# Neighbourhood attention inside a fused block: TensorE in a written order, six filling units a step

## The chip, the core and the metric

The kernel runs on one NeuronCore of a Trainium2 chip. A core has five engines that run side by side: TensorE (PE in the profile, with its weight loads as PEld), VectorE (DVE), ScalarE (ACT), GpSimd (POOL) and SyncE (SP), which here issues the transfers. Each engine takes its instructions in the fixed order in which the program was written out for it; between engines there are semaphores. The metric is the time of one execution on the device, in microseconds (us), the median of several runs; lower is better.

## The reference, cut to what matters

One layer of a diffusion backbone on 1024 latent tokens (a grid of 16 rows by 64 columns) with 256 context tokens, 1024 features, all in fp32. The stage that matters here is the neighbourhood attention, beside the wide projections that are independent of it:

```python
h = modulate(rmsnorm(x, norm1_g), sh1, sc1)
q, k, v = ...                      # 8 heads of 64, q and k normalised
s_loc = einsum(q, k_window) * scale + bias      # 8 x 16 window round each query
s_ctx = einsum(q, k_ctx) * scale                # all 256 context keys
p = softmax(concat([s_loc, s_ctx]))             # one softmax over both
o_na = p_loc @ v_window + p_ctx @ v_ctx
og, m_a, m_b = h @ w_in[:, ...]                 # 2560 further columns: "dense" products
o_g = gla_bidir(...)                            # chunked linear attention, next stage
mix = (sigmoid(m_a) * (o_na @ w_br_na) + sigmoid(m_b) * (norm(o_g) * silu(og) @ w_br_gla)) @ w_out
```

## The kernel before

Every fp32 product is made of three products of fp32r parts (high and low halves). The stages follow each other: input norms and projections, neighbourhood attention (NA), linear attention (GLA), merge of the two branches, output projection, feed-forward network.

**The filler.** The 2560 columns of og, m_a and m_b need 320 *units*: a unit is three products of 128x512 into the bank `psd` (one feature block `k` of one output tile). They depend on nothing in the attention, so a generator (`dense_units`, `fill(n)`) hands them out n at a time wherever TensorE would otherwise wait. Eight units make a tile, which ACT (and DVE for og) takes out of PSUM as `std`. NA and GLA take fixed numbers of units; what is left over is written out in one block by `fill(1000)` (line 1008) between GLA and the merge.

**NA.** 8 heads x 4 steps, a step being two query tiles of 128 ("piece", `c2`). What a step does is set by the words of `ORD` (line 48), read in `na_out` (lines 754 to 766). `tN`: group N of four 128x128 blocks of the probabilities `pb` is transposed on TensorE into a bank `pt`; ACT casts it to `phl` (high part) and DVE subtracts for the low part. `aN`: the value products of that group, `pv<-phl,vhl`. A step has 9 or 10 blocks, so groups 0 and 1 are full and group 2 has one or two. `l`: the logits of the **next** step (`cp` for the context, `lp` for the window, two tiles each). `w`: its softmax: DVE takes the minimum `mn` and, with the bias, `pb` and `mx`; ACT takes four exponentials with their sums; DVE adds and inverts the sums (`rs`); DVE scales the first tile's `pb` and ACT the second's. `fN`: N units. `p`: transposes of the next head's keys and queries (`tpk`, `tpq`), two groups in the first two steps of a head, one in the third, none in the fourth. `pt`, `tpk` and `tpq` share two PSUM banks (tag "T", `bufs=2`), which come free when DVE has read them. At the end of a step ACT and DVE add the two halves of `pv` (`t1n`), and DVE adds the result into `oT`, whose two inputs lie in SBUF.

**What sets the order.** With `in_order(True)` each TensorE instruction is tied to the one written before it. With `in_order(False)` a scheduler chooses when the program is built, by its own estimate of times; the chosen order is then as fixed on the chip as a written one. GLA and the merge are in a written order in both kernels; NA's is `NAO` (line 792), and before NA comes the start: keys and queries of head 0, eight units (`FSTART`, line 790), the first logits and softmax (line 791).

```python
prepare(0, 9)
prepare(1, 1)
fill(FSTART)
cur = na_weights(0, 0, *na_logits(0, 0))
in_order(NAO)
for s, (h, c2) in enumerate(steps):
    ...
    cur = na_out(h, c2, steps[s + 1] if s + 1 < len(steps) else None, *cur)
```

**After GLA.** The merge needs `ona_d` (NA's output, written to HBM) and `w_na` back in SBUF as four and two pages of high and low parts (lines 1083 to 1088): a page is loaded by SP into `raw` (three buffers, shared with GLA), cast by ACT (`w_hi`), and subtracted on DVE (`w_lo`). Its products go to the bank `psb`.

Of the kernel before, what the change touches and what calls it, by code (L numbers as in the profile page):

```python
# [43 lines left out]
OORD = (0, 0, 1, 1)  # L44
FIN = 2
NPB = 3
NAO = False
ORD = "f2 t0 l t1 w f1 a0 t2 f1 a1 f1 a2 p".split()
FG = 0
FSTART = 8  # L50
PREP = (2, 2, 2, 0)
# [37 lines left out]
def hybrid_block_kernel(  # L89
# [35 lines left out]
    class Ordered:  # L125
# [4 lines left out]
        def in_order(self, on):  # L130
            self.on, self.last = on, None
# [502 lines left out]
    with ExitStack() as sn:  # L634
# [48 lines left out]
        def na_logits(h, c2):  # L683
            bias, vhl, qh, ql, ks = heads[h]
            cp = nps.tile([P, 2, TC], F32, tag="C", name="cp")
            for ci in range(2):
                cs_ = slice((2 * c2 + ci) * P, (2 * c2 + ci + 1) * P)
                PE.matmul(cp[:, ci], qh[:, cs_], ks[:, T:], start=True, stop=False)
                PE.matmul(cp[:, ci], ql[:, cs_], ks[:, T:], start=False, stop=True)
            lps = []  # L690
            for ci in range(2):
                c = 2 * c2 + ci
                k0, k1 = max(0, c - 1), min(8, c + 2)
                nl = (k1 - k0) * P
                lp = nps.tile([P, 512], F32, tag="L", name="lp", bufs=2)
                cs_ = slice(c * P, (c + 1) * P)
                PE.matmul(lp[:, 0:nl], qh[:, cs_], ks[:, k0 * P:k1 * P], start=True, stop=False)
                PE.matmul(lp[:, 0:nl], ql[:, cs_], ks[:, k0 * P:k1 * P], start=False, stop=True)
                lps.append((lp, k0, k1, nl))
            return cp, lps  # L700
# [32 lines left out]
        def na_out(h, c2, ahead, blocks, pbs, ns):  # L733
# [19 lines left out]
            res = None  # L753
            for op in ORD:
                if op[0] == "f":
# [35 lines left out]
# [3 lines that stand above are left out]
# [930 lines left out]
```

## Time and profile before

| | us |
|---|---|
| median of 3 runs (1607.38 to 1611.16) | 1608.04 |
| the profiled execution's own time | 1602.4 |
| its span, first to last instruction | 1600.6 |
| start of NA's transposes to the last value product | 355.2 to 595.3 |
| GLA with its units | 595.3 to 734.2 |
| the left-over units | 734.2 to 759.6 |
| merge, from its first product | 759.6 |

TensorE is busy in 96% of the span. Busy time of TensorE is a model of pipelined products, whose ends overlap; so a waiting time that the profile shows is somewhat shorter than what the engine lost.

### The profile page before, as it was taken

Reading aid. Unit: us, or ns where it says so; the run is one execution under the profiler, and the core shown is the slowest. Engines: PE = TensorE matmul, PEld = TensorE weight load, DVE = VectorE, ACT = ScalarE, POOL = GpSimd, SP = SyncE. Lnnn points to the kernel's source line nnn. Section 1 sums busy time; section 2 is a strip of 40 time slices with the busy share of each in tenths; the row PEclk is TensorE's granted clock in tenths of the full one; section 3 lists DMA queues with packets and bytes.
Section 4 is the critical chain, followed back from the end, with each engine's and each line's share of the span. In section 5 each row is a group of like instructions: output and inputs, shape, how many; then the busy total and the mean of one; then the engine's idle time right before and its main releaser. Section 6 shows DMA issues by size and latency. Waiting matters only on the chain.

```text
span 1600.6 us, 21607 instructions
## 1 busy us (share of the span) xinstructions
PE 1535.6 (96%) x7884; PEld 1257.4 (79%) x7884; DVE 1017.5 (64%) x1598; ACT 637.8 (40%) x1221; POOL 516.4 (32%) x340
## 2 busy tenths in 40 slices
PE   6998999999989999999999999799999999999998
PEld 4777777888878787778878887688888888877886
DVE  5745567228877865543684678866666665768356
ACT  4333453248777763122212434233333333344442
POOL 3333000023121211210221421655555555245444
PEclk9999999999999999999999999999999999999999
DMA  9456576454333327415652343433333333874342
GB/s 339 127 174 210 170 250 211 154 156 124 112 105 94 98 88 228 151 67 204 225 182 66 106 132 106 138 115 116 99 99 99 99 112 119 269 250 145 99 145 99
DMA packets 171668, 235.50 MB, mean 147 GB/s; under 512 B 15581, under 2 KB 105629, under 8 KB 171561
## 3 DMA queue, kind: packets, MB, share of 16 engines
q1 hardware_dynamic: 171560, 234.11, 45.2%
q8 instruction: 62, 1.02, 0.3%
q14 instruction: 46, 0.37, 0.1%
HBM read 167.83 MB, written 66.24 MB: 146 GB/s over the span
## 4 chain that ended last, share of the span: by engine, by line
PE 71%; DVE 12%; DMA 5%; issue 5%; ACT 4%; POOL 2%; SPq 1%; ACTq 0%; DVEq 0%; POOLq 0%
PE psdn L137 10%; PE psj L137 9%; PE psd L137 9%; PE fZ L137 7%; PE fW L137 7%; PE fX L137 6%; PE pso L137 5%; PE psb L137 4%; PE fY L137 4%; PE pv L137 2%; PE pt L137 1%; SPq L137 1%; ACT pb L137 1%; POOL r L249 1%; PE mp L137 1%
## 5 line engine op out<-in xcount | busy, mean ns | idle before, releaser
L137 PE MATMUL psdn<-wd,a 128*128 128x512 f32 x924 | 213.4, 392 | 5.0 <-ACT u L137 2.0
L137 PEld LDWEIGHTS psdn<-wd,a 128*128 128x128 f32 x924 | 174.0, 189 | 44.3 <-DVE a L137 3.4
L211 POOL TENSOR_TENSOR w_P<-sc,w_P 128x512 fp32r<-128x512 f32 x80 | 119.4, 1495 | 126.3 <-ACT w_P L137 126.3
L137 PE MATMUL fZ<-T,w_P 128*128 128x512 f32 x528 | 128.3, 392 | 8.5 <-DVE u L137 8.5
L137 PE MATMUL psd<-hh,w_hi 128*128 128x512 f32 x320 | 133.6, 418 | 0.0
L211 POOL TENSOR_TENSOR w_lo<-raw,w_hi 128x1024 fp32r<-128x1024 f32 x24 | 57.6, 2404 | 219.9 <-ACT w_hi L137 195.1
L137 PE MATMUL psd<-hh,w_lo 128*128 128x512 f32 x320 | 128.1, 400 | 0.0
L137 PE MATMUL psj<-w_hi,hh 128*128 128x512 f32 x320 | 127.0, 399 | 0.7 <-ACT hh L137 0.6
L137 PE MATMUL psd<-hl,w_hi 128*128 128x512 f32 x320 | 127.3, 398 | 0.0
L137 PE MATMUL psj<-w_lo,hh 128*128 128x512 f32 x320 | 126.0, 394 | 0.0
L137 PE MATMUL psj<-w_hi,hl 128*128 128x512 f32 x320 | 125.3, 395 | 0.3 <-DVE r L137 0.3
L137 PEld LDWEIGHTS fZ<-T,w_P 128*128 128x128 f32 x528 | 100.2, 190 | 29.9 <-issue 8.9
L211 POOL TENSOR_TENSOR w_P<-raw,w_P 128x512 fp32r<-128x512 f32 x56 | 87.3, 1559 | 78.2 <-ACT w_P L137 69.0
L137 ACT CAST w_P<-sc 128x512 fp32r<-128x512 f32 x88 | 54.0, 621 | 129.4 <-PE fZ L137 65.6
L137 DVE TENSOR_TENSOR a<-ar,a 128x512 fp32r<-128x512 f32 x77 | 66.6, 875 | 61.2 <-ACT a L137 61.1
L137 PE MATMUL fX<-B,w_P 128*128 128x512 f32 x432 | 103.8, 389 | 0.0
L249 POOL TENSOR_TENSOR r<-r,nhalf 128x8 f32<-128x8 f32 (+1 forms) x40 | 51.6, 1293 | 161.8 <-DVE r L137 161.8
L137 ACT CAST a<-ar 128x512 fp32r<-128x512 f32 x77 | 47.9, 622 | 117.1 <-PE psdn L137 62.8
L137 PEld LDWEIGHTS fX<-B,w_P 128*128 128x128 f32 x432 | 81.1, 188 | 16.8
L137 ACT CAST w_hi<-raw 128x1024 fp32r<-128x1024 f32 x56 | 58.3, 1051 | 54.4 <-PE psj L137 15.3
L137 DVE SCALAR_TENSOR_TENSOR t1f<-t1f,u 128x512 f32<-128x512 f32 x66 | 62.1, 941 | 20.1 <-ACT t1f L137 19.0
L137 PEld LDWEIGHTS psj<-w_hi,hh 128*128 128x128 f32 x320 | 60.8, 190 | 14.7 <-ACT hh L137 2.0
(267 smaller groups left out, 3478.4 us busy)
## 6 DMA issues: line engine op xcount, KB each, us to landing
wm<-in_w_mod_dram SPq DMA_DIRECT2D x48, 512.0 KB
raw<-in_w_in_dram SPq DMA_DIRECT2D x40, 512.0 KB
ar<-s_d SPq DMA_DIRECT2D x77, 256.0 KB
raw<-in_w_gate_dram SPq DMA_DIRECT2D x22, 512.0 KB
raw<-in_w_up_dram SPq DMA_DIRECT2D x22, 512.0 KB
s_d<-t1f SPq DMA_DIRECT2D x44, 256.0 KB
s_d<-sa SPq DMA_DIRECT2D x33, 256.0 KB
xt<-in_x_dram SPq DMA_DIRECT2D x16, 512.0 KB
```

Of the source, the lines that this page charges most:

```text
L137: r = op(*args, **kw)
L211: return (lo_eng or DVE).tensor_tensor(lo, src, hi.bitcast(F32), op=ALU.subtract)
L249: POOL.tensor_tensor(r, r, nhalf[:, 0:w], op=ALU.pow)
```

## The change

Two constants. NA's TensorE instructions are now tied to each other in the written order, and the order itself is another one: the step begins with a group's transposes in place of two units, a unit or two stand between a group's transposes and its value products, the next head's transposes come before the last four units, and there are six units a step where there were five. By count, 200 units are handed out up to the end of NA (8 + 32 x 6) where it was 168, and 5 are left for `fill(1000)` where it was 37.

```diff
-NAO = False
-ORD = "f2 t0 l t1 w f1 a0 t2 f1 a1 f1 a2 p".split()
+NAO = True
+ORD = "t0 f1 l w t1 f1 a0 t2 f2 a1 p f2 a2".split()
```

TensorE at the start of NA, before: head 0's keys (`tpk`) and queries (`tpq`) are transposed with units (`psd`) put between them.

```order
L137 MATMUL tpk<-ident,kd 128x128 x8
L137 MATMUL psd<-hl,w_hi 128x512
L137 MATMUL psd<-hh,w_lo 128x512
L137 MATMUL psd<-hh,w_hi 128x512
L137 MATMUL psd<-hl,w_hi 128x512
L137 MATMUL psd<-hh,w_lo 128x512
L137 MATMUL tpk<-ident,kd 128x128 x2
L137 MATMUL psd<-hh,w_hi 128x512
L137 MATMUL psd<-hl,w_hi 128x512
L137 MATMUL psd<-hh,w_lo 128x512
L137 MATMUL tpq<-ident,qd 128x128 x4
```

The same place now, from the first transpose to the first transpose of probabilities.

```order
L137 MATMUL tpk<-ident,kd 128x128 x10
L137 MATMUL tpq<-ident,qd 128x128 x8
L137 MATMUL cp<-ks,qh 128x256
L137 MATMUL lp<-ks,qh 128x256
L137 MATMUL lp<-ks,qh 128x384
L137 MATMUL cp<-ks,ql 128x256
L137 MATMUL cp<-ks,qh 128x256
L137 MATMUL cp<-ks,ql 128x256
L137 MATMUL lp<-ks,ql 128x256
L137 MATMUL lp<-ks,ql 128x384
L137 MATMUL pt<-ident,pb 128x128 x4
```

Ahead of the first `pt` TensorE had 20 and a third units; now it has the eight of `FSTART`, all of them ahead of the first `tpk`, and none after it.

ScalarE in the second step of a head (here head 1; the two groups of transposes of this step are `tpk` and `tpq`), before. `phl` 128x512 are the casts of groups 0 and 1, `phl` 128x256 that of group 2, `pb<-pb,rs` the second tile's scaling; the first tile's two exponentials stand ahead of these rows.

```order
L137 CAST phl<-pt 128x512 x2
L137 ACTIVATE pb,sums<-cp,mx 128x256
L137 ACTIVATE pb,sums<-pb,mx 128x384
L137 ACTIVATE std<-psd 128x512
L137 CAST phl<-pt 128x256
L137 ACTIVATE pb<-pb,rs 128x640
L137 ACTIVATE ks<-tpk,kg_sb 128x256
L137 COPY t1n<-pv 128x256
L137 ACTIVATE qh<-tpq,qgn 128x512
```

The same step now.

```order
L137 CAST phl<-pt 128x512 x2
L137 ACTIVATE pb,sums<-cp,mx 128x256
L137 ACTIVATE pb,sums<-pb,mx 128x384
L137 ACTIVATE pb,sums<-cp,mx 128x256
L137 ACTIVATE pb,sums<-pb,mx 128x384
L137 ACTIVATE std<-psd 128x512
L137 ACTIVATE pb<-pb,rs 128x640
L137 CAST phl<-pt 128x256
L137 ACTIVATE ks<-tpk,kg_sb 128x256
L137 ACTIVATE qh<-tpq,qgn 128x512
L137 COPY t1n<-pv 128x256
```

Group 2's cast has moved behind the whole softmax and its scaling; so it stands in the second steps of the heads 0, 1, 2, 5 and 6; in those of heads 3 and 4 and in the first steps of a head it comes straight behind the four exponentials.

On TensorE, 111 products stand between the last transposes of GLA and the merge's first `psb` before, and 15 now; the order of ACT, DVE and SP there has not changed but for the `std` and its store of each tile that went.

## Rows read from the trace of the kernel before

**Rows 1.** The page's head: the span.

```profile
span 1600.6 us, 21607 instructions
```

**Rows 2.** Windows by stage: length, busy time (count) of each engine, clock, DMA.

```profile
342.70:355.20 12.50, 11.80 (x65) 9.37 (x65) 7.24 (x16) 7.80 (x17) 6.20 (x4) 1.00 0.85 250
355.20:595.30 240.10, 230.47 (x1421) 195.24 (x1421) 188.94 (x449) 185.20 (x478) 48.15 (x24) 1.00 0.33 101
595.30:734.20 138.90, 132.86 (x1188) 107.79 (x1187) 71.53 (x136) 36.41 (x64) 24.67 (x12) 0.98 0.45 150
734.20:759.60 25.40, 25.40 (x114) 21.06 (x113) 8.30 (x8) 5.46 (x7) 0.00 (x0) 1.00 0.71 249
```

**Rows 3.** The chain that ended last, 730 to 765 us: start, length, what.

```profile
734.41 25.18 PE psd L137 x111
```

**Rows 4.** What TensorE waited for, 355.2 to 595.3: total, times, longest.

```profile
PE pv L137 <- DVE phl L137: 8.2, 9, 2.0
PE pt L137 <- DVE pb L137: 1.0, 2, 0.8
```

**Rows 5.** TensorE's groups in NA: busy, mean ns, idle before.

```profile
L137 PE MATMUL psd<-hh,w_hi 128*128 128x512 f32 x149 | 61.9, 415 | 0.0
```

**Rows 6.** TensorE in order of time, start of NA: start, length, what.

```profile
342.76 1.09 PE L137 MATMUL tpk<-ident,kd 128*128 128x128 f32 x8
...
349.08 0.46 PE L137 MATMUL lp<-ks,ql 128*128 128x256 f32 x2
...
355.20 1.06 PE L137 MATMUL pt<-ident,pb 128*128 128x128 f32 x8
```

**Rows 7.** TensorE's groups, 335.5 to 355.2.

```profile
L137 PE MATMUL psd<-hh,w_hi 128*128 128x512 f32 x21 | 8.5, 403 | 0.0
```

**Rows 8.** All engines in order of time, one step of NA (450 to 459 us).

```profile
449.99 2.38 POOL L211 TENSOR_TENSOR w_lo<-raw,w_hi 128x1024 fp32r<-128x1024 f32 x1 [5.67 <-ACT w_hi L137]
...
450.58 2.07 DVE L137 TENSOR_TENSOR oT<-t1n 64x256 f32<-64x256 f32 x1
...
454.42 0.38 ACT L137 CAST phl<-pt 128x256 fp32r<-128x256 f32 x1 [3.05 <-PE pt L137]
454.45 0.64 PE L137 MATMUL pv<-phl,vhl 128*128 128x256 f32 x4
454.68 0.48 ACT L137 ACTIVATE pb<-cp,mx 128x256 f32<-128x256 f32 x1
...
454.95 0.42 DVE L137 TENSOR_TENSOR phl<-pt,phl 128x256 fp32r<-128x256 f32 x1
...
456.70 0.20 ACT L137 ACTIVATION_READ_ACCUMULATOR pb<-pb,mx 128x1 f32 x1
...
456.93 0.16 DVE L137 TENSOR_TENSOR rs<-sums 128x2 f32<-128x2 f32 x1 [1.56 <-ACT pb L137]
...
457.72 0.84 ACT L137 ACTIVATE pb<-pb,rs 128x640 f32<-128x640 f32 x1
```

**Rows 9.** DVE's groups in NA: the sum into oT.

```profile
L137 DVE TENSOR_TENSOR oT<-t1n 64x256 f32<-64x256 f32 x31 | 22.7, 731 | 1.0
```

**Rows 10.** SP's queue after GLA: NA's output comes back.

```profile
735.92 1.46 SPq L137 DMA_DIRECT2D raw<-ona_d  x2
...
738.91 0.65 SPq L137 DMA_DIRECT2D raw<-ona_d  x1
```

**Rows 11.** ACT there: high parts of those pages.

```profile
742.09 1.05 ACT L137 CAST w_hi<-raw 128x1024 fp32r<-128x1024 f32 x1 [3.63 <-DMA raw<-ona_d]
...
745.87 1.05 ACT L137 CAST w_hi<-raw 128x1024 fp32r<-128x1024 f32 x1 [0.92 <-DMA raw<-ona_d]
```

**Rows 12.** DVE there: the last page's low part.

```profile
746.96 1.23 DVE L137 TENSOR_TENSOR w_lo<-raw,w_hi 128x1024 fp32r<-128x1024 f32 x1 [1.25 <-ACT w_hi L137]
```

**Rows 13.** Windows round an early gap of TensorE (idle 147.3 to 151.6).

```profile
145.00:150.50 5.50, 2.32 (x11) 1.59 (x9) 2.02 (x4) 0.69 (x2) 1.64 (x1) 1.00 0.92 320
150.50:157.50 7.00, 5.86 (x14) 4.65 (x15) 4.22 (x7) 3.86 (x6) 2.90 (x2) 0.51 0.37 122
```

## The prediction

> **What bounds the kernel now.** I read the windows by stage first, then TensorE's waits inside the attention, then the stretches on both sides of it in order of time. The span is 1600.6 us [rows 1], and TensorE is hardly ever idle where the change works. The left-over units after GLA run without a gap: 111 products in 25.18 us [rows 3], so 0.227 us a product and 0.68 us a unit. In the attention, 240.1 us long, TensorE is busy for 230.5 [rows 2]: 9.6 us idle, nearly all of it ahead of value products and of transposes, waiting for DVE [rows 4]. Its 32 steps hold 149 units [rows 5], 101 us at the undisturbed pace. So there is little room: an engine that is busy nearly all the time is not made faster by handing it the same units earlier. What the reader should keep from this: the units are conserved. 32 units (21.8 us) leave the stretch after GLA and are done in the attention; the time changes only by what TensorE's idle time changes. I therefore sum idle time and nothing else.
>
> **The start of the attention.** Before, 21 units run between 335.5 and 355.2 us [rows 7], and the chain of head 0 (transposes of keys at 342.76, last logits at 349.08, softmax, first probabilities transposed at 355.20 [rows 6]) is hidden behind them. Its length is a matter of ACT, DVE, POOL and transfers, which the change leaves alone. Now eight units stand ahead of the first transpose and none behind it: TensorE has 12.3 units less in that stretch, and they are done later, after the chain. 12.3 x 0.68 = **8.4 us** of new idle time. Below: if the chain shortens because no unit's `std` lies between its steps, I give it at most 1 us back. Above: nothing, since the chain's instructions are the same.
>
> **The steps.** I lay one second step of a head out from its first `pt` (time 0), from rows. Transposes stand 0.1 us apart (eight in 0.8 before the last begins [rows 6]); four value products take 0.64 with the last one's own 0.28 in it, so 0.12 apart [rows 8]; I use 0.12 for the logits of 256 and an estimate of 0.18 for those of 384. TensorE: group 0 until 0.40, unit 1.08, logits 1.56 and 2.28, group 1 2.68, unit 3.36, value products 3.84, group 2 4.04, two units 5.40, value products 5.88, the two `tpk` 6.08. Then comes `tpq`, which needs the bank of group 2, because both banks "T" are taken (one by group 2, one by `tpk`). That bank comes free so: group 1 is cast until about 3.5, the four exponentials take 2.2 us (454.68 to 456.90), the sum 0.16 and its inverse as much with their hand-overs 0.4, the scaling 0.84, the cast of group 2 0.38, its low part 0.42 [rows 8]: 3.5 + 2.2 + 0.4 + 0.84 + 0.38 + 0.42 = 7.75, with the signal to TensorE 7.9. TensorE waits 1.8 us, and behind the `tpq` in its queue stand the two units which could have filled that time, and the last value products. Before, group 2 was cast ahead of the scaling, and units stood ahead of `tpq` where it was late.
>
> This order of ACT holds in the second steps of five heads: 5 x 1.8 = 9.0. In the two other second steps the scaling falls out of the sum (7.0 against 6.1 to 6.3), 0.7 each, 1.4; the first step of a head has the same wait for its second `tpk` by the same sum, but TensorE arrives 0.2 later: 0.6 x 7 = 4.2. Heads 0 to 2 have the og units, whose `std` costs DVE a pass ahead of group 2's low part: 0.7 x 3, and casts of dense weights ahead of the exponentials in some steps: together 3. Third and fourth steps come out even (the first tile's scaling ends at about 7.1, the step at 7.2 to 7.9).
>
> There remain DVE's late sums. `oT` alone takes 0.42 us in its shortest forms, but 2.07 while POOL ran a weight cast from 449.99 to 452.37 [rows 8], and 0.73 in the mean of 31 [rows 9]: 9.6 us in all, which is where the 8.2 us of waits for `phl` come from. Behind `oT` stands group 0's low part in DVE's queue in the new order too, but now a unit, four logits and four more transposes lie ahead of the value products that need it: I halve it, 5. Sum of step waits: 9.0 + 1.4 + 4.2 + 3 + 5 = 22.6, less the 9.6 of before: **13.0 us**. Below: every bank free in time and `oT` fully covered, -9.6. Above: the waits delay DVE and ACT in turn and the first group of the next step is late as well, 0.5 us more in each of 32 steps and no halving: 22.6 + 16 + 5 = 44, so +34. I take the middle value because it goes by queues that are written down.
>
> The Trainium skill (SBUF — State Buffer, Who interferes with whom) says that a VectorE instruction with two SBUF inputs shares a port with GpSimd and is held for the whole of a GpSimd instruction that reads SBUF. The 2.07 us row agrees with it. By that rule alone, with POOL at work for 48 of 240 us, 32 sums would meet some 6 passes of up to 2.4 us: 7 us rather than my 5, so the sum would be 2 us higher.
>
> **After GLA.** Five units instead of 37: the merge's first product stands 3.4 us behind the last transposes, at 737.6 in the clock of before. But NA's output comes back late: its second and third page are asked for at 735.92, the fourth at 738.91 [rows 10], when GLA's last buffers come free; their high parts begin at 742.09 and 745.87 [rows 11], and the last low part ends at 748.19 [rows 12]. The first bank of the merge reads all four pages, so it ends at about 748.7 instead of 737.6 + 2.7 = 740.3: **8.4 us** that lay behind the left-over units. These loads are tied to GLA's end, which does not move against them. Below, with fewer stores beside them: 6. Above: 9.5.
>
> **The clock.** After a gap of 4.3 us (147.3 to 151.6) the granted clock was 0.51 for 7 us [rows 13], which is the lower level, 1.2 GHz. At the start (TensorE does 2.7 us of work in 12.5) and after GLA (a gap of about 5 us) I expect the same, while TensorE partly waits anyway: **2 us** for both. Below 0; above, if the waits of 1.8 us drop it in many heads too, 10.
>
> GLA has the same units at the same places (it starts one whole weight chunk, 32 units, later in their row), so nothing. The attention takes one chunk of weights more: two loads, two ACT casts and two POOL passes of 2.4 us [rows 8], each chunk now due every 5.3 steps, some 45 us apart, in which SP and POOL (48 of 240 us busy) have time; nothing, unless a load waits behind another in SP's queue, when the strict order would hold all of TensorE.
>
> **Sum.** 8.4 + 13.0 + 8.4 + 2 = 31.8 us. Against the profiled execution: 1602.4 + 31.8 = 1634; the median of the runs shown is 5.6 above that execution, so I add the 31.8 to 1608: **1640 us**, 2.0% slower.
>
> **The rivals.** (A) The written order runs clean: TensorE's waits in the steps stay about where they were, because ACT and DVE have 1 us more per step to be in time. For it: ACT is busy 185 and DVE 189 of 240 us, so a longer step gives slack. Against it: a bank is waited for, not an engine. 8.4 + 0 + 8.4 + 1, or less: +5 to +20, 1613 to 1628. (B) It is worse: the waits of 1.8 us lower the clock and carry over into the next step's first group: +45 to +65, 1653 to 1673. (C) Faster: the attention has hidden room. Of its 1421 TensorE instructions [rows 2] 447 are products of units, 101 us; 90 are logits of 384, 16 us; the other 884 at 0.11 to 0.12 take 97 to 106. That is some 218 of 240 us, so up to 22 us could be taken by units, if waits and loose pace vanish. That needs the order to be free of waits for banks; then 8.4 + 8.4 - 22 = -5, 1603. It decides for faster when the steps lose less than 22 - 17 = 5 us together, 0.16 us a step. (D) The gains and losses cancel within 0.3% (4.8 us).
>
> The Trainium skill (Perfetto Trace Analysis, Identifying the Most-Contended Engine) holds that TensorE's room is read from the weight loads' busy share and not from the products'. By it the attention (195.2 of 240.1 us, 81%) is nearly as full as the gapless stretch after GLA (21.1 of 25.4, 83%), room for 4 us and not 22, which makes (C) come out at +13.
>
> **Chances.** Main case, +20 to +45: 0.59. (A) 0.17, (B) 0.10, (C) 0.08, (D) 0.06. What this measurement tells from no change is about 0.3%. So slower 0.86, same 0.06, faster 0.08. The range leaves out (C), (D) and half of (B) with a little of (A): 1615 to 1660; the main case's own is 1628 to 1653.
>
> **What would show it.** The new profile should have: a first stretch with TensorE idle 8 to 9 us between the first `tpk` and the first `pt`; waits of `tpk` and `tpq` for DVE's `phl`, 12 to 18 us in all, which do not exist now; `psb` waiting for `w_hi` or `w_lo` after GLA for some 8 us; the attention about 45 us longer, from its first `pt` to its last value product, and 22 less after GLA. If `tpk` and `tpq` wait for nothing, the step part is wrong, and (A) or (C) is right. If the first `psb` does not wait, the pages came earlier than their buffers let me think.

## The result

| | before | after |
|---|---|---|
| median of 4 runs each (us) | 1607.71 | 1642.7 |
| ratio, 95% interval | | 1.0236, 1.0213 to 1.0258 |
| span of the profiled execution (us) | 1600.6 | 1638.9 |

The change makes the kernel 2.4% slower, 35 us; the prediction was 1640 us. The page of the changed kernel, head and the row of the granted clock:

```profile
span 1638.9 us, 21630 instructions
...
PEclk9999999989999999999899999899999999999999
```

The windows by stage of the changed kernel, cut at TensorE's own rows (first unit, first `pt`, last value product, last transposes of GLA, first and last `psb`); columns as in [rows 2]:

```profile
337.11:356.16 19.05, 10.96 (x51) 8.30 (x50) 6.55 (x14) 8.10 (x18) 6.05 (x4) 0.83 0.83 250
356.16:647.68 291.52, 265.66 (x1558) 230.30 (x1558) 190.13 (x450) 192.10 (x485) 52.78 (x26) 0.97 0.30 90
647.68:784.21 136.53, 131.08 (x1190) 106.58 (x1189) 69.31 (x137) 34.85 (x63) 19.91 (x10) 0.99 0.43 145
784.21:787.74 3.53, 3.53 (x19) 2.93 (x17) 3.15 (x4) 0.00 (x0) 0.00 (x0) 1.00 0.54 172
787.74:889.00 101.26, 92.91 (x385) 73.63 (x383) 69.19 (x73) 24.13 (x26) 22.30 (x8) 0.95 0.62 207
```

The same cuts of the kernel before:

```profile
335.68:355.20 19.52, 18.82 (x96) 15.00 (x95) 7.93 (x17) 8.99 (x19) 6.20 (x4) 1.00 0.81 240
355.20:595.01 239.81, 230.18 (x1420) 194.95 (x1420) 188.94 (x449) 185.20 (x478) 48.15 (x24) 1.00 0.33 101
595.01:734.14 139.13, 133.09 (x1189) 108.02 (x1189) 71.47 (x136) 36.41 (x64) 24.67 (x12) 0.98 0.45 150
734.14:759.42 25.28, 25.28 (x114) 20.95 (x113) 8.36 (x8) 5.46 (x7) 0.00 (x0) 1.00 0.71 250
759.42:849.55 90.13, 87.69 (x384) 71.65 (x383) 64.29 (x68) 20.68 (x23) 21.78 (x8) 1.00 0.54 181
```

Stages that hold different numbers of units are compared by taking 0.68 us a unit off; what is left is called the rest of a stage. Its change splits into idle time (length less busy) and pace (busy less units: a lower clock, or products that fit together less well).

| stage | units before, after | rest before, after | change | idle | pace |
|---|---|---|---|---|---|
| start | 20.3, 8 | 5.7, 13.6 | +7.9 | +7.4 | +0.5 |
| attention | 148.3, 192 | 138.9, 160.9 | +22.0 | +16.2 | +5.8 |
| GLA | 114.3, 115 | 61.4, 58.3 | -3.1 | -0.6 | -2.5 |
| after GLA to the last `psb` | 37, 5 | 90.3, 101.4 | +11.1 | +5.9 | +5.2 |

Sum +37.9: 28.9 of idle time and 9.0 of pace. The spans differ by 38.3; what is left lies outside these stages (1.4 more ahead of the first unit, 1.2 less behind the last `psb`).

What TensorE waited for in the attention:

```profile
PE tpq L137 <- DVE phl L137: 11.0, 7, 3.0
PE tpk L137 <- DVE phl L137: 6.9, 3, 3.3
PE pv L137 <- DVE phl L137: 6.2, 7, 3.1
...
PE pt L137 <- DVE ks L137: 1.1, 2, 0.6
```

Before there were only waits of value products and of `pt` [rows 4]. Now 17.9 us are waits of `tpk` and `tpq` for the bank that holds group 2. They lie where ACT's queue put them. For each step I read what stands on ACT between the cast of group 1 and that of group 2 (in the last row: ahead of the cast of group 1), and beside it the wait in the trace:

| steps | ahead of the cast on ACT | wait (us) |
|---|---|---|
| second steps of heads 3, 4 | four exponentials | 0.75, 0.72 (`tpq`) |
| second steps of heads 0, 1, 5 | exponentials and scaling | 1.42, 1.40, 1.53 (`tpq`) |
| second steps of heads 2, 6 | those and a weight cast `w_hi` | 2.98, 2.18 (`tpq`) |
| first steps of heads 1, 5 | exponentials and a weight cast | 3.30, 3.19 (`tpk`) |
| last step of head 3 (group 1's cast) | a weight cast and exponentials | 3.12 (`pv`) |

The five long ones all have a weight cast in the queue. In three of them ACT also sat idle for its transfer (2.79, 2.47 and 2.68 us); in the second steps of heads 2 and 6 it waited 0.35 us and nothing, and the cast's own 1.05 us is what was added. One of the three, all engines in order of time:

```profile
392.60 2.42 POOL L211 TENSOR_TENSOR w_lo<-raw,w_hi 128x1024 fp32r<-128x1024 f32 x1 [5.52 <-ACT w_hi L137]
...
395.04 0.38 SPq L137 DMA_DIRECT2D raw<-in_w_in_dram  x1
...
399.21 1.04 ACT L137 CAST w_hi<-raw 128x1024 fp32r<-128x1024 f32 x1 [2.79 <-DMA raw<-in_w_in_dram]
400.16 0.47 ACT L137 ACTIVATE pb<-cp,mx 128x256 f32<-128x256 f32 x1
...
402.26 0.25 ACT L137 CAST phl<-pt 128x128 fp32r<-128x128 f32 x1
...
402.61 0.28 DVE L137 TENSOR_TENSOR phl<-pt,phl 128x128 fp32r<-128x128 f32 x1
...
402.94 0.66 PE L137 MATMUL tpk<-ident,kd 128*128 128x128 f32 x4 [3.30 <-DVE phl L137]
```

ACT sits 2.79 us idle for a transfer of weights that nobody needs yet; four exponentials and group 2's cast stand behind it, and TensorE waits 3.3 us. The transfer is late because it is asked for late, at 395.04: the profile puts SP's wait down to GpSimd's pass over the page before, which ended at 395.02. The view of ACT's waits gives the sum of such idle time in the attention, before and after (one row each):

```profile
ACT w_hi L137 <- DMA raw<-in_w_in_dram: 2.4, 3, 1.2
```

```profile
ACT w_hi L137 <- DMA raw<-in_w_in_dram: 11.2, 6, 2.8
```

The clock shows in windows cut where TensorE's pace changes: before the stretch, in it and behind it for the wait above, one more in the attention, and one after GLA.

```profile
402.94:404.30 1.36, 1.36 (x8) 1.23 (x9) 1.29 (x3) 1.36 (x3) 0.00 (x0) 1.00 0.14 42
404.30:407.71 3.41, 3.41 (x13) 2.86 (x12) 2.17 (x5) 1.12 (x3) 0.00 (x0) 0.50 0.50 137
407.71:411.00 3.29, 3.29 (x24) 3.08 (x23) 2.63 (x7) 1.47 (x5) 0.00 (x0) 1.00 0.00 0
...
598.86:602.27 3.41, 3.41 (x13) 2.84 (x12) 1.12 (x3) 0.69 (x1) 0.00 (x0) 0.50 0.51 196
793.42:803.66 10.24, 8.62 (x17) 5.26 (x18) 4.36 (x4) 4.62 (x5) 0.00 (x0) 0.50 1.01 382
```

Half of full speed, 1.2 GHz, for 3.41 us: two products of a unit begin 0.42 us apart in it (404.41 and 404.83) and 0.24 behind it (409.51 and 409.75). Four of the five long waits are followed by such a stretch; the waits of 0.7 to 1.5 us are not.

Start and end of the stretch, TensorE in order of time:

```profile
343.88 1.09 PE L137 MATMUL tpk<-ident,kd 128*128 128x128 f32 x8 [1.17 <-DMA kd<-k_d]
...
356.16 0.45 PE L137 MATMUL pt<-ident,pb 128*128 128x128 f32 x1 [5.69 <-DVE pb L137]
...
793.90 0.80 PE L137 MATMUL psb<-w_hi 128*128 128x512 f32 x1 [5.33 <-ACT w_hi L137]
```

Head 0's chain takes 12.28 us from its first transpose, as before (12.44 [rows 6]), now uncovered. The merge waits for NA's pages. The second and third are asked for at 786.77, the fourth at 789.67, and their casts on ACT begin 6.0 to 10.3 us behind 786.77 (6.2 to 10.0 before [rows 10, 11]):

```profile
792.81 1.04 ACT L137 CAST w_hi<-raw 128x1024 fp32r<-128x1024 f32 x1 [4.27 <-DMA raw<-ona_d]
...
797.08 1.04 ACT L137 CAST w_hi<-raw 128x1024 fp32r<-128x1024 f32 x1 [1.37 <-DMA raw<-ona_d]
```

### The profile page after: what moved, and what is told of

It reads as the page before. It is cut to its first block, busy times and chain, and to the rows that moved or that the text cites. A ratio compares the mean times of both kernels' runs of the same rounds, so it can differ in the third digit from the quotient of the medians.

```text
span 1638.9 us, 21630 instructions
## 1 busy us (share of the span) xinstructions
PE 1545.1 (94%) x7884; PEld 1268.8 (77%) x7884; DVE 1016.8 (62%) x1598; ACT 640.1 (39%) x1221; POOL 517.6 (32%) x340
## 4 chain that ended last, share of the span: by engine, by line
PE 66%; DVE 10%; DMA 9%; ACT 6%; issue 5%; POOL 3%; SPq 1%; ACTq 0%; DVEq 0%; POOLq 0%
PE psdn L137 9%; PE psd L137 8%; PE psj L137 8%; PE fZ L137 7%; PE fW L137 7%; PE fX L137 6%; PE pso L137 5%; PE psb L137 4%; PE fY L137 4%; DMA raw<-in_w_in_dram 2%; ACT pb L137 2%; DMA q_d<-st 1%; SPq L137 1%; DMA wm<-in_w_mod_dram 1%; PE pt L137 1%
## 5 line engine op out<-in xcount | busy, mean ns | idle before, releaser
L137 PE MATMUL psd<-hh,w_hi 128*128 128x512 f32 x320 | 141.4, 442 | 0.0
L137 ACT CAST w_hi<-raw 128x1024 fp32r<-128x1024 f32 x56 | 58.4, 1049 | 69.3 <-DMA raw<-in_w_in_dram 25.3
L137 PEld LDWEIGHTS psj<-w_hi,hh 128*128 128x128 f32 x320 | 61.3, 192 | 14.6 <-ACT hh L137 1.8
```

The costliest lines, as they stand in the source:

```text
L137: r = op(*args, **kw)
```

## The experiments

All times are ratios to the kernel before, timed on the same chip, with 95% intervals; the changed kernel has 1.0236, and 0.1% is 1.6 us. "Rest" is as above. What each stage kept:

| run | ratio | start | attention | GLA | after GLA |
|---|---|---|---|---|---|
| before | 1 | 5.7 | 138.9 | 61.4 | 90.3 |
| the change | 1.0236 | 13.6 | 160.9 | 58.3 | 101.4 |
| e1 | 1.0076 (1.0053 to 1.0099) | 6.2 | 140.9 | 56.8 | 102.5 |
| e2 | 1.0140 (1.0114 to 1.0166) | 12.9 | 150.4 | 62.4 | 90.6 |
| e3 | 1.0182 (1.0156 to 1.0208) | 13.9 | 151.5 | 58.8 | 102.1 |
| e4 | 1.0141 (1.0119 to 1.0163) | 13.7 | 147.4 | 58.3 | 100.2 |
| e5 | 1.0194 (1.0166 to 1.0221) | 11.7 | 159.9 | 58.0 | 102.8 |
| e6 | 1.0174 (1.0158 to 1.0189) | 14.2 | 159.6 | 65.5 | 90.0 |
| e9 | 1.0027 (1.0006 to 1.0047) | 6.0 | 146.3 | 61.3 | 88.7 |
| e10 | 1.0110 (1.0088 to 1.0132) | 14.3 | 145.5 | 58.0 | 102.0 |
| e11 | 1.0018 (1.0004 to 1.0032) | 5.7 | 142.2 | 66.6 | 90.3 |
| e12 | 1.0037 (1.0023 to 1.0050) | 10.9 | 146.3 | 56.1 | 90.4 |
| e13 | 1.0068 (1.0052 to 1.0085) | 10.6 | 149.8 | 59.0 | 89.2 |
| e14 | 1.0089 (1.0075 to 1.0104) | 11.0 | 142.6 | 58.1 | 101.8 |

**e1: six units and the new words, in the scheduler's order.**

```diff
-NAO = True
+NAO = False
```

> The new words of ORD with six units a step, but the scheduler chooses TensorE's order in the attention, as before the change. Theory of the prediction (the loss comes from the written order: no units behind head 0's transposes, banks waited for in queue order; the stretch after GLA loses by the count of units): the start is covered again, TensorE's idle time in the attention is about 10 us as before, only the wait after GLA stays, about 8.4 us and its clock. 1612 to 1620 us. Rival (the six units and the new words themselves are too much for ACT, DVE and the weight loads, whoever orders them): the waits in the attention stay near 26 us, 1630 to 1645 us.

As the first theory said. Start and attention are back but for 0.5 and 2.0 us; what is lost lies after GLA (12.2). The attention, in windows, and ACT's waits for weights in it:

```profile
357.62:620.67 263.05, 249.82 (x1513) 214.79 (x1513) 189.29 (x448) 189.75 (x483) 53.09 (x26) 0.99 0.33 100
```

```profile
ACT w_hi L137 <- DMA raw<-in_w_in_dram: 10.3, 6, 3.2
```

ACT waits for weights nearly as long as in the changed kernel (11.2), yet TensorE is idle 13.2 us here and 25.9 there. So late weights on ACT cost what they do because a written order stands behind them.

31.3 units more than before took 23.2 us more, 0.74 a unit. So this order found no hidden room, which was the ground of rival (C). The Trainium skill (Perfetto Trace Analysis, Identifying the Most-Contended Engine) holds that TensorE's room is judged by the weight loads' busy share (and by useful work) and not by the products' busy time; the trace agrees, with a share of 81% before [rows 2].

**e2: the old words, five units, in a written order.**

```diff
-ORD = "t0 f1 l w t1 f1 a0 t2 f2 a1 p f2 a2".split()
+ORD = "f2 t0 l t1 w f1 a0 t2 f1 a1 f1 a2 p".split()
```

> The old words of ORD, five units a step, with TensorE tied to the written order. 37 units are left after GLA, as before. Bank theory (a strict order makes tpk and tpq wait for group 2's bank, whatever the words): start 10.3 units short, 7 us; waits of tpk and tpq in the attention 10 to 18 us; nothing after GLA: 1622 to 1632 us. Rival (the new words, with p ahead of the last units, make the waits): start 7 us alone, 1612 to 1616 us.

The size came out (start 7.2, attention 11.5), not the place: no `tpk` or `tpq` waits; the value products wait 14.5 us for DVE's low parts, and `pt` 3.8 us for a bank. A strict order costs with the old words and five units a step too, at whatever stands in it when ACT and DVE are late. With e1, where the new words and six units cost 2.0 us in the attention, this makes the order the cause there and at the start.

```profile
PE pv L137 <- DVE phl L137: 14.5, 13, 1.9
...
PE pt L137 <- DVE ks L137: 3.8, 7, 2.1
```

**e3: dense weights cast by GpSimd** (from the second chunk on, `NHP = 1`).

```diff
-        c = ACT.copy(hi, src)
+        c = hi_eng.tensor_copy(hi, src) if hi_eng is not None else ACT.copy(hi, src)
...
-            w = load_w(wp, w_in[:, c0:c0 + 256], KT, 256, lo_eng=POOL, after=GATE[ch])
+            w = load_w(wp, w_in[:, c0:c0 + 256], KT, 256, lo_eng=POOL, hi_eng=POOL if ch >= NHP else None, after=GATE[ch])
```

> The changed kernel with the high parts of the dense weights (128x1024, from the second chunk on) cast by GpSimd in place of ACT. In the changed kernel ACT sits idle ahead of these casts for 11.2 us in 6 places (2.4 before the change), waiting for the transfer of the weights, with the next step's exponentials behind them in its queue; the five long waits of TensorE (2.3 to 3.5 us, 15.6 us in all) stand right there, and four of the five stretches of half clock in the attention follow them. Theory 1 (these casts hold ACT's queue): the long waits fall to 1.7 us or less and the clock stays up; 9 to 14 us less, 1629 to 1634 us. Theory 2 (that of the prediction: group 2's cast comes late by its place behind exponentials and scaling, transfers play no part): 0 to 4 us less, 1639 to 1643 us.

The attention gets 9.4 us back (5.2 of idle time, 4.2 of pace), 0.5% in the ratio: theory 1 in the main. Of the five long waits four fell to under 1.5 us; the fifth is still 2.48, and two others are over 2. The bank is still waited for:

```profile
PE tpq L137 <- DVE phl L137: 9.5, 7, 2.5
...
PE tpk L137 <- DVE phl L137: 5.3, 4, 2.2
PE pv L137 <- DVE phl L137: 1.5, 4, 0.7
```

No transfer is left in ACT's queue, and two things remain. In the second steps of heads 0 and 1 the scaling stands ahead of group 2's cast, and `tpq` waits 2.08 and 1.55 us: the order on ACT is a cause of its own. In the other two waits of over 2 us a pass of GpSimd over the weights held DVE; one of them:

```profile
437.01 2.35 POOL L211 TENSOR_TENSOR w_lo<-raw,w_hi 128x1024 fp32r<-128x1024 f32 x1
...
437.34 2.03 DVE L137 TENSOR_TENSOR rs<-sums 128x2 f32<-128x2 f32 x1 [1.14 <-ACT pb L137]
...
439.63 0.66 PE L137 MATMUL tpk<-ident,kd 128*128 128x128 f32 x4 [2.18 <-DVE phl L137]
```

The sum `rs`, 0.16 us in rows 8, lasts until GpSimd's pass is over, and group 2's low part stands behind it on DVE. Nine of the 31 sums took 0.44 to 2.03 us, and each ended within 0.02 us of a GpSimd pass; in the changed kernel none took over 0.5. So the weight casts in ACT's queue cost rather more than 9.4 us; how much no run shows.

**e4: p behind the last units.** The words end in `f2 p a2` in place of `p f2 a2`.

> The changed kernel with the word p moved behind the last two units (f2 p a2 in place of p f2 a2): tpk and tpq come 1.36 us later and the two units fill the time in which the bank of group 2 comes free. Bank theory: the ten waits of tpk and tpq (17.9 us) lose up to 1.36 us each, 7 to 9 us are left; two or three stretches of half clock go with them: 10 to 14 us less, 1629 to 1633 us. Rival (the units are only moved: the wait returns ahead of the last value products or of the next step's first transposes, which need the same banks): less than 4 us, 1639 to 1643 us.

The bank waits of `tpk` and `tpq` fall from 17.9 to 2.4 us and the attention by 13.5 us, more than the bank theory said. Part came back, as the rival said, as waits of the next step's first transposes for the bank of `tpk`: 7.5 us, where the changed kernel has 1.1. ACT's waits for weights fell as well, from 11.2 to 3.9 us, so e4 does not tell the two causes apart.

```profile
PE pt L137 <- DVE ks L137: 7.5, 9, 1.0
...
PE tpq L137 <- DVE phl L137: 2.4, 2, 1.3
```

**e10: w behind t2.** `ORD` is `t0 f1 l t1 f1 a0 t2 w f2 a1 p f2 a2`. Group 2's cast then stands behind one or two exponentials, or none, and never behind the scaling.

> The changed kernel with the word w moved behind t2, no TensorE instruction moved. On ACT, group 2's cast then stands ahead of two or all four exponentials and of the scaling. Theory of the prediction (bank T is held because this cast is queued behind the whole softmax): the waits of tpk and tpq fall from 17.9 us to 5 or less, except where a late transfer of weights holds ACT ahead of the cast (5 us more); the softmax is up to 1 us later and the next step's first transposes wait for pb, 0 to 10 us in all: 5 to 14 us less than the changed kernel, ratio 1.015 to 1.020. Rival (the bank is late through the whole load on ACT and DVE, in whatever order): the waits move from tpk and tpq to pt one for one, ratio 1.022 to 1.028.

`tpq` no longer waits at all, `tpk` 3.8 us; the attention gets 15.4 us back, the ratio came below the range. ACT still waits 8.8 us for weights, so this gain is not that of the weights but of the cast's place; the 3.8 us lie in the three steps where a weight cast still stands ahead of group 2's. Of the rival a part is true: the next bank in the row is waited for.

```profile
PE pt L137 <- DVE ks L137: 10.2, 10, 2.6
...
PE tpk L137 <- DVE phl L137: 3.8, 3, 1.7
```

**e5: twelve units more at the start.** `FSTART` is 20, and the second `f2` gives one unit in the last twelve steps.

> The changed kernel with twelve units more ahead of the attention (FSTART 20 in place of 8) and one less in each of the last twelve steps (the second f2 gives one), so that 5 units are left after GLA as before. Theory (head 0's chain has only eight units, 12.3 too few): start and units together lose 7 to 8 us, TensorE's wait for the first probabilities falls from 5.7 us to under 0.5; in the last twelve steps the six bank waits grow by up to 0.68 us each, 2 to 4 us back: 4 to 6 us less than the changed kernel, ratio to the kernel before about 1.020. Rival (the units delay the chain itself, through ACT and DVE, which take them out of PSUM): the first probabilities come 4 us or more later than now and nothing is won, ratio 1.023 to 1.026.

Only 1.9 us were won at the start. The scheduler put the units ahead of the chain, and SP's queue shows what they pulled forward:

```profile
331.79 7.70 SPq L137 DMA_DIRECT2D raw<-in_w_in_dram  x2
...
341.10 0.64 SPq L137 DMA_DIRECT2D kd<-k_d  x1
```

Two weight loads now stand ahead of head 0's keys, which were asked for at 338.81 in the changed kernel.

**e14: 21 units laid into the chain by hand.** One behind each group of transposes, eight behind the logits, and one less in each of the last thirteen steps.

```diff
-                    if PE.on and n < 9:
-                        fill(FG)
+                    if PE.on and (h == 0 or n < 9):
+                        fill(FG if h else 1)
...
-        prepare(0, 9)
+        in_order(NAO); fill(FSTART - 1)
+        prepare(0, 6)
         prepare(1, 1)
-        fill(FSTART)
         cur = na_weights(0, 0, *na_logits(0, 0))
-        in_order(NAO)
+        fill(8)
```

> The changed kernel with 21 units at the start in place of 8, laid between head 0's transposes (one behind each group) and behind its logits (eight), and one less in each of the last thirteen steps; 5 are left after GLA as before. Theory (the term of the start, 8.4 us, is cover that stands at the wrong place, and the run with FSTART 20 put it ahead of the chain instead of behind its steps): from the first unit to the first probabilities 19 to 21 us for 21 units (19.1 for 8 now), 7 to 8 us won there, 2 to 4 us given back by five-unit steps: ratio 1.018 to 1.021. Rival (the chain is stretched by whatever is put beside it, 25.3 us as with FSTART 20): 1.022 to 1.025.

At the start the same loads were pulled ahead of the keys, and the whole 5.0 us of idle time (25.28 less 20.26) is that one wait; behind it nothing is idle:

```profile
347.10 0.48 PE L137 MATMUL tpk<-ident,kd 128*128 128x128 f32 x1 [5.02 <-DMA kd<-k_d]
```

So the units do cover the chain where they lie beside it, as they do in e1, e9 and e11 (rest 5.7 to 6.2). As a time this is what the rival said (25.3 us for the stretch), for another reason. What neither theory gave is the attention: 18.3 us less with nearly the same words. ACT's order had moved: the scaling stands ahead of group 2's cast in no step, and ACT waits 2.5 us for weights in place of 11.2.

```profile
PE pv L137 <- DVE phl L137: 7.1, 6, 2.6
PE tpq L137 <- DVE phl L137: 1.8, 4, 0.9
```

e5 has nearly the same units in each step, and its `tpq` waits are short too, but its attention won only 1.0 us. ACT waits 9.2 us for weights there, and other waits of TensorE took the place of the old ones (of the 9.8 us below, 4.1 lie at the end of the start):

```profile
PE pt L137 <- DVE pb L137: 9.8, 4, 4.8
...
PE tpq L137 <- DVE phl L137: 3.7, 5, 1.2
```

```profile
579.96 1.64 DVE L137 COPY dec<-X 128x16 f32<-128x16 f32 x1 [1.65 <-DMA X<-ex_d]
...
583.49 1.09 PE L137 MATMUL pt<-ident,pb 128*128 128x128 f32 x4 [4.81 <-DVE pb L137]
```

The longest has the same form as on ACT: a copy for the next stage waits on DVE for its transfer, the softmax's scaling stands behind it, and `pt` waits 4.81 us. The words of `ORD` alone thus don't fix the loss.

**e6: 21 units left after GLA.** The second `f2` gives one unit in the last sixteen steps.

> The changed kernel with one unit less in each of the last sixteen steps, so that 21 units are left after GLA in place of 5. Theory (NA's output comes back some 11 us after GLA's end, by GLA's buffers, and 5 units do not cover that): the 11.1 us that the stretch from GLA's end to the last psb lost, its units taken out, go away altogether; the bank waits of eight first and second steps grow by up to 0.68 us, 3 to 5 us back: 6 to 8 us less than the changed kernel, ratio about 1.019. Rival (the merge is held by something that the units delay with it, such as stores of the same queue): psb waits as long behind 21 units as behind 5, no gain, ratio 1.023 to 1.027.

The stretch after GLA is whole again (90.0), at full clock. GLA itself lost 7.2 us: its transposes wait 3.5 us for a load of keys, and its clock is 0.95.

**e9: scheduler's order, p last, five units, GpSimd casts.** `NAO = False`, words `t0 f1 l w t1 f1 a0 t2 f2 a1 f1 p a2`, the cast of e3.

> The scheduler's order again, with the new words (p behind all units), five units a step, 37 left after GLA, and the high parts of the dense weights cast by GpSimd. If the written order is the cause of the losses before and in the attention and the count of units that of the loss after GLA, this has neither: within 0.4% of the kernel before. With ACT free of the wait for weights (2.4 us in the kernel before) it may be 0 to 5 us faster: ratio 0.997 to 1.002. Rival (the new words themselves cost): 1.004 or more.

No better than before and a little above the expected range: 7.4 us more in the attention, where ACT no longer waits for weights; the value products wait 10.9 us for DVE (8.2 before).

**e11: e1 with 21 units left.** `NAO = False` on e6.

> The new words with the scheduler's order and six units a step in the first half of the attention, five in the second half, so that 21 units are left after GLA in place of the 5 of the first run of this kind (1.0076). Theory (all that run lost was the uncovered return of NA's output, 12.2 us): 11 to 13 us less than that run, ratio 0.998 to 1.002; no psb waits for w_hi or w_lo. Rival (the loss after GLA comes with the order before it, not with the count of units): ratio 1.005 to 1.008.

As expected: 0.6% less than e1. The stretch after GLA is whole, the attention too but for 3.3 us; GLA loses 5.2, with 3.3 us of waiting for the same load as in e6.

**e12: a written order without the three losses.** The start of e14, `w` behind `t2`, words `t0 f1 l t1 f1 a0 t2 w f1 a1 p f2 a2`, 24 units left.

> A written order throughout, with the three losses taken out: at the start 21 units, one behind each group of head 0's transposes and eight behind its logits; w behind t2; five units a step (t2 w f1 a1 p f2 a2), so that 24 are left after GLA. If the three terms (start 7.9, bank waits 15 of 22, after GLA 11.1) are independent, the run with w behind t2 (1.011) loses 0.7% + 0.5% more: ratio 0.997 to 1.004, the part above 1.000 for the bank waits that one unit less a step lays bare. Rival (a strict order costs by itself, since it can't give way to late transfers and GpSimd passes): 1.006 to 1.012.

1.0037, inside the range at its upper end. The terms did not add up one by one: the start keeps its wait for keys (5.2 of rest) and the attention 7.4, where `pt` waits 8.5 us for a bank, while GLA is 5.3 shorter than before.

**e13: e12 with the GpSimd casts of e3.**

> The kernel before this one in the list with the high parts of the dense weights cast by GpSimd from the second chunk on, so that no transfer holds ACT's queue. If ACT's waits for weights (8.8 us in the run with w behind t2) reach TensorE as they did in the changed kernel: 3 to 8 us less, ratio 0.994 to 1.000. Rival (with group 2's cast early they are covered, and GpSimd's longer passes slow DVE's sums instead): same or 1 to 4 us more.

The rival: 0.3% slower. DVE is busy 196.2 us in the attention (191.0 in e12), and `pt` waits 7.2 us for `pb` (3.3). The 31 sums `rs` took 10.2 us in place of 6.4: four took 0.62 to 2.00 us and ended within 0.02 us of a GpSimd pass over the weights, as in e3. The sums into `oT` did not lengthen (17.7 us, 18.6 in e12). How much of the 0.3% this makes is not shown. No version beat the kernel before.

## Why the prediction was right, and where not

The forecast of 31.8 us stands against 35.0 in the medians and 38.3 in the profiled spans. Behind each heading is the forecast.

**Start** (8.4): 7.9, of which 7.4 is idle time. e1 gives it back by order alone; the chain's length didn't change.

**Step waits** (22.6 after, 13.0 net): 25.7 and 16.2. The bank behind ACT's queue was the cause: shown by e10, where the cast comes earlier and the weights are still late, and less cleanly by e4. The sum for the second steps came out (10.4 forecast, 11.0 measured) partly by luck: with the scaling ahead and no weight cast the waits were 1.40 to 1.53 where 1.8 was forecast, with a weight cast 2.18 and 2.98; without the scaling 0.72 and 0.75 against 0.7. The 4.2 for first steps was wrong in kind: five of the seven waited 0.4 us or nothing, two over 3 us, for a weight cast whose data hadn't landed. That is the step that failed in the text: one chunk of weights more was priced at "nothing, unless a load waits behind another in SP's queue". The price was in ACT's queue: taking the weight casts out of it (e3) gives 9.4 us back with the clock. This and the 15.4 of e10 are together more than the 22.0 that were lost, so the two causes share waits. Of the 5 for DVE's late sums, 3.1 is left when the long wait is taken off. The 7 us that the prediction worked out by the Trainium skill's rule on the shared port (SBUF — State Buffer, Who interferes with whom) are not borne out in the changed kernel; e3 and e13 show such holds, on `rs`.

**After GLA** (8.4): 5.9 idle and 5.2 of pace. e6 and e11, with 21 units, remove both, so it is cover and nothing else; part of what it gives is lost again in GLA (7.2 in e6, 5.2 in e11), where a load of keys comes late.

**Clock** (2): 9.0 of pace net, the mis-sized term: 0.5 at the start, 5.8 in the attention, 5.2 after GLA, 2.5 less in GLA, which had two half-speed stretches before and one now (GLA was priced at nothing). To read all of it as the clock's is an estimate: the five half-speed stretches of the attention hold 17.4 us of busy time, half of it 8.7, so 2.9 of that was won elsewhere. Idle time alone was forecast at 29.8 and is 28.9, but its parts missed by 1.0 less (start), 3.2 more (steps) and 2.5 less (after GLA): that they cancel is luck.

Of the signs that were named, the bank's waits came as said (17.9 us, 12 to 18 forecast), and 21.8 us left the stretch after GLA. TensorE is idle 6.9 us between the first `tpk` and the first `pt` (8 to 9), `psb` waits 6.4 us for `w_hi` and `w_lo` (some 8), and the attention is 51.7 us longer (45).

**The rivals.** (A) falls with the 17.9 us of bank waits. (B) was right that waits lower the clock, wrong that they carry over: in the steps no `pt` waits for `pb`. (C) lacks its room: e1 found none, though 5.5 us of bank waits are left in it, and the attention's busy time less its units, 129.3 us before, is over 127 in every run. (D) falls with the time. What stays open is why the scheduler places ACT's scaling before the cast in one build and behind it in another; what the cast's place is worth is shown by e10.

## What to carry to other kernels

When one engine is tied to a written order, read the queues of the others again: what the attention lost was decided by what ACT had ahead of a small cast, and by a transfer at the head of its queue, as the same late weights cost little under the scheduler's order (e1). Units moved from one place to another are worth the idle time that they cover and the clock that it would have cost: count what each end needs (20 at the start; 21 after GLA were enough) before handing them out elsewhere, and price a wait with the clock that follows it.

## What was not expected of the hardware

Waits of 2.2 to 3.3 us in a busy attention were followed in four places of five by a stretch of 3.41 us at half clock. After GLA a wait of 5.3 us was followed by 10.24 us at 1.2 GHz, although TensorE was busy for 8.62 of them. DVE's sum `rs`, 0.16 us in rows 8, took 2.03 us in e3 and ended with a pass of GpSimd over a page of weights.
